# Last two layers with the gated-linear-attention block in the head, attention in finer steps, and other durations in the program's clock

## The chip, the cores and the metric

The kernel runs on 1 core of one Trainium2 chip, in one launch. The metric is device time in microseconds: the median of three runs before is 2298.22 us (2297.33 to 2300.84).

## The reference

Four layers over 256 tokens of width 1024. The first two (kind "a") have a mixer of four branches and a gated feed-forward part; the last two (kind "b") have another mixer, cross-attention to a memory, and a squared-ReLU part. What the change touches is the mixer of kind "b", and the attentions of both kinds:

```python
def mixer_block(h, ...):                      # kind "b", 256 tokens
    zin = h @ w_in
    (cq, ckv, kpe, sg_uv, gq, gk, gv, g_lr, g_og,
     dq, dk, dv, da, db, dz, gates) = jnp.split(zin, splits, axis=-1)
    o_a = mla_branch(cq, ckv, kpe, ...)       # causal attention, 4 heads
    o_b = spatial_gating_branch(sg_uv, ...)   # u * (tril(w_s) @ layernorm(v)), gelu before
    o_c = gla_branch(gq, gk, gv, g_lr, g_og, ...)   # gated linear attention, chunks of 64
    o_d = deltanet_branch(dq, dk, dv, da, db, dz, ...)
    branches = jnp.stack([o_a, o_b, o_c, o_d], axis=2)
    proj = jnp.einsum('bsnw,nwd->bsnd', branches, w_branch)
    gate = jax.nn.sigmoid(gates).reshape(b, s, N_BRANCH, D_MODEL)
    merged = jnp.sum(gate * proj, axis=2)
    return merged @ w_out
```

The mixer of kind "a" has a state-space branch and three softmax attentions of eight heads (fox, moba, dsa). Everything is in float32.

## The kernel before

Each large product is done in three: an fp32 operand is split into `hi` (rounded to fp32r) and `lo` (the rest), and TensorE multiplies lo x hi, hi x lo and hi x hi (`mm3`, L652). The small products of the branches are plain fp32 matmuls. Weights come in chunks of two 128-row tiles by up to 512 columns, 512 KB, in the order that `plan` (L67) lists and from which they are also laid out in memory. SyncE loads a chunk into one of 4 raw buffers (`load`, L486); `high` (L496) writes hi on ScalarE; `low` (L509) writes lo on VectorE, frees the raw buffer and asks for the next load. There are 8 pairs of hi and lo, and preparation runs at most 5 chunks ahead (`LOOK`).

The program writes out the order of all instructions of every engine itself; each engine then works through its own list in order. The main thread is the list of blocks of large products (`block`, `g1`, `g2`, `head`). Around it run lanes, Python generators, one for each branch ("A", "B", "C", "S", "X"), and short spawned chains such as an evacuation. A lane puts out instructions up to its next `yield`. The order comes from a model of the chip, a clock for each engine (`Model`, L303): `Engine.cost` (L372) gives each instruction a duration, `dma` (L428) gives one to a load, and a result can be read some 200 ns after its end. After 3 to 12 matmuls of the main thread `tick` (L635) is called. It puts out the next step of a lane when, by that clock, TensorE has come to the time at which the lane's last results are ready; lanes wait while VectorE or ScalarE is more than `BACKLOG` (2750 ns) behind TensorE. `advance` (L521), called in `tick`, puts out at most one `low` and one `high`: when the chunk is needed within 4000 ns of matmuls, or when the engine is not more than 1500 ns behind TensorE. The program is written twice; the first pass only finds when each chunk is needed. So other durations change the order and nothing else. `flush(key)` puts out all steps left of the chains with a key at once. Buffers of the branches are taken from an arena of 19968 words for each partition (`F`); when it is full, `relieve` puts out steps of other lanes early.

`attention` (L855) is one generator for all softmax attentions of a mixer. A step takes two heads: it multiplies the probabilities of the pair before last with v, transposes those of the last pair on TensorE and copies them to SBUF, multiplies q and k of this pair, reduces the rows on VectorE, takes exponentials on ScalarE, and then a reciprocal (128x4) and four multiplications on VectorE. There is one `yield` for each step.

In `layer_b` (L1635) the blocks are A (latents of the attention, low-rank gate, deltanet's scalars; 440 columns) and E (spatial gating, 512 columns), both in the head, and then those of `MORDER` (L64): B (keys and queries of gated linear attention, 256), qk (512), F (its values and output gates, 512), v (256) and dz (256). `head` (L714) works through the first 128 tokens of both blocks ahead of the second 128, since these are normalised meanwhile. After E each half gets `gelu` (L1739); lane "S" (`sgu`, L1765) first flushes these chains and then does spatial gating; lane "A" is `mla` with the attention of four heads; lane "C" is `gla` (L1813), set off after block F; lane "B" is deltanet (`dn`), set off after v. `gla` needs the low-rank gate first (softplus on VectorE), B's keys and queries then, and F's values only near its end, where it waits for `placed`. `mix` (L1400) then asks for the branches in the order 1 (spatial gating), 0, 2, 3 (`ORDER2`), with two gate blocks for each.

Of the kernel before, what the change touches and what calls it, by code (L numbers as in the profile page):

```python
# [59 lines left out]

ORDER1 = (2, 1, 3, 0)
ORDER2 = (1, 0, 2, 3)
MIDDLE = dict(B=("gq", "gk"), qk=("dq", "dk"), v=("dv",), F=("gv", "gog"), dz=("dz",))
MORDER = ("B", "qk", "F", "v", "dz")  # L64


def plan(layer):  # L67
# [33 lines left out]
            else:  # L101
                cb(f"d{j}{c}", "w_ffn_out", (l,), (256 * j, 256 * j + 256), [(c * 512, c * 512 + 512)])
    else:
        for name, parts in (("A", ("ckv", "kpe", "cq", "glr", "da", "db")), ("E", ("sg",)),
                            *((n, MIDDLE[n]) for n in MORDER)):
            cb(name, "w_in_2", (l,), full, [W2[p] for p in parts])
        g0 = W2["gates"][0]
# [244 lines left out]
class Engine:  # L352
# [19 lines left out]
    def cost(self, fn, outs, ins, kw):  # L372
        if self.name == "PE":
            if fn == "transpose":
                return 109.0
            m, n = ins[0].free_size(), ins[1].free_size()
            one = max(m / 1.2, n / 2.4) + 2
            return one if ins[0].dtype == F32R else max(112.0, max(2 * m / 1.2, 4 * n / 2.4))
        n = max(a.free_size() for a in outs[:1] + ins)
        psum = any("PSUM" in str(a.space) for a in ins + outs)  # L380
        ptr = sum(1 for a in ins if a.free_size() == 1) if n > 1 else 0
        if self.name == "ACT":
            return (94 if psum else 147) + n / 1.2 + 93 * (ptr + (len(outs) > 1))
        if self.name == "POOL":
            return 300 + 167 * n if kw.get("op") == OP.pow else 150 + 2.1 * n
        if fn in ("tensor_copy", "tensor_scalar", "memset") and not psum:
            return (n / 2 + 66) / 0.96 + 61 * ptr
        return (n + 66) / 0.96 + 61 * ptr + (1600 * n / 256 if fn == "reciprocal" else 0)


class Kern:
# [36 lines left out]
    def dma(self, out, in_):  # L428
        if self.due is not None:
            self.nc.sync.dma_start(out, in_)  # L430
        if "SB" in str(out.space):
            self.model.op("DMA", out.nbytes() / 360.0, 2000.0, [out], [])

    def act(self, out, in_, f=AF.Copy, scale=1.0, bias=None, accum=None):
        kw = {}
# [419 lines left out]
    def attention(self, heads, qk, sel, bias, v, dst, done):  # L855
# [16 lines left out]
        for i in range(n + 2):  # L872
# [15 lines left out]
            if 1 <= i <= n:  # L888
                ps, pts = st.pop(("p", i - 1)), []
                for p in ps:  # L890
                    b = self.bank()
                    for c in range(3):
                        self.tr(b[:, 128 * c:128 * c + 128], p.a[:, 128 * c:128 * c + 128])
                    pt = F.alloc(384, "pt")
                    self.copy(pt.a, b[:, :384])
                    self.fbank(b)
                    p.free()
                    pts.append(pt)
                st[("pt", i - 1)] = pts
            if i < n:  # L900
                qks = [qk(2 * i + j) for j in range(2)]
                bb = [self.bank() for _ in range(2)]
# [16 lines left out]
                for j in range(2):  # L919
                    for t, (a, c) in enumerate(tiles):  # L920
                        self.V.tensor_tensor_reduce(out=ps[j].a[:, a:c], in0=bb[j][:, 2 * a:2 * a + c - a], in1=bias[:, a:c],
                                                    scale=1.0, scalar=3e38, op0=OP.add, op1=OP.min,
                                                    accum_out=nv[:, 0, j, t:t + 1])
                    self.fbank(bb[j])
                    for t, (a, c) in enumerate(tiles):
                        self.act(ps[j].a[:, a:c], ps[j].a[:, a:c], AF.Exp, scale=-1.0, bias=nv[:, 0, j, t:t + 1],
                                 accum=nv[:, 1, j, t:t + 1])
                self.V.reciprocal(nm.a[:, 8:12], nm.a[:, 4:8])
                for j in range(2):
                    for t, (a, c) in enumerate(tiles):  # L930
# [704 lines left out]
    def layer_b(self, l, hT, nxt, pr, early):  # L1635
# [127 lines left out]
                bce.free()  # L1763

        def sgu():  # L1765
            self.flush("sg")
            m = Mat(self, 2, 256, "yT")
            for t in range(2):
                b = self.bank()
# [10 lines left out]
            ys[1].append(m)  # L1780
            flags.add(1)

        self.head(L, [("A", 440, ev_A), ("E", 512, ev_E)], hT)


        def convs(name, c0, n):
            for g in range(n):
# [2 lines left out]
                        [(256 * g, 256 * g + 128), (256 * g + 128, 256 * g + 256)], 4, g == n - 1)  # L1790
                self.spawn(self.conv(b, [cwt[:, c0 + 2 * g + j] for j in range(2)], None,
                                     cv.v(3, 512)[:, c0 // 2 + g]), "conv")
        self.lane("S", sgu())
        self.lane("A", mla())

        gq, gk = F.alloc(256, "gq"), F.alloc(256, "gk")
        def gate_ev(dst, b, src, norm):
            th = F.alloc(256, "gth")
# [10 lines left out]

        def ev_dz(t, b):  # L1810
            self.spawn(gate_ev(zg.v(2, 256)[:, t], b, b[:, 0:256], n_dn), "dz")

        def gla():  # L1813
            while len(given) < 2:
# [378 lines left out]

        cv = F.alloc(6 * 256, "cv")
        cvv = cv.v(6, 256)
        gv, gg, zg = F.alloc(512, "gv"), F.alloc(512, "gg"), F.alloc(512, "zg")
        for name in MORDER:
            if name == "qk":
                convs("qk", 0, 2)
# [2 lines left out]
            elif name == "B":  # L2202
                b = self.bank()
                self.g2([b[:, 0:256], b[:, 256:512]], L, "B", hT, [(0, 128), (128, 256)], 4)
                self.act(gq.a, b[:, 0:256], AF.Copy, scale=32 ** -0.5)
                self.act(gk.a, b[:, 256:512])
                self.fbank(b)
            elif name == "F":
                self.block(L, "F", hT, 512, ev_F)
                self.lane("C", gla())  # L2210
            else:
                self.block(L, "dz", hT, 256, ev_dz)
            placed.add(name)
# [467 lines left out]
```

## Time and profile before

| | us |
|---|---|
| median of the runs | 2298.22 |
| profiled execution, its own time | 2296.01 |
| its span, first to last instruction | 2294.2 |
| TensorE busy | 2237.2 |
| VectorE busy | 1526.5 |
| ScalarE busy | 1074.2 |
| GpSimd busy | 271.2 |
| mean granted TensorE clock | 0.991 |

PE is TensorE's matmuls, PEld its weight loads, DVE VectorE, ACT ScalarE, POOL GpSimd, SP SyncE. Nearly all instructions stand under line 362, the helper that issues them, so groups are told apart by tile names and shapes: `rt` holds split operands, `raw` weights as loaded, `ft` and `qt` the branches' buffers, `bank` PSUM. DVE `rt<-raw,rt` is `low`, ACT `rt<-raw` is `high`. A plain fp32 matmul stands as two records. Matmuls overlap in the pipeline, so the mean duration of one is longer than the time from one to the next. The first two layers take the span up to some 1149 us, the third starts there, and the last at some 1718 us.

### The profile page before, as it was taken

The numbers are of one execution on the slowest core, as the hardware profiler recorded it, in microseconds if no ns is written. First come the engines' busy times: TensorE is split into PE (matmuls) and PEld (weight loads), VectorE is DVE, ScalarE is ACT, GpSimd is POOL, SyncE is SP. The second block draws the span as 40 slices with busy tenths as digits, with TensorE's granted clock in tenths as the row PEclk, the third lists the DMA queues.
The fourth block names the chain that finished last, engine by engine and source line by source line (L and its number), as shares of the span: only waits on it lengthen the run. The fifth ranks groups of instructions, "written<-read, shape, count | busy, mean of one in ns | idle before, by whom it ended". The sixth has DMA issues, their size and how long they took to land.

```text
span 2294.2 us, 40097 instructions
## 1 busy us (share of the span) xinstructions
PE 2237.2 (98%) x16244; PEld 2020.1 (88%) x16244; DVE 1526.5 (67%) x2509; ACT 1074.2 (47%) x1695; POOL 271.2 (12%) x244
## 2 busy tenths in 40 slices
PE   7999999999999999999999999999999999999998
PEld 6888998999787899889988899988988889998897
DVE  7786657555888655755588867555557887755554
ACT  4554544444455444544454345444545433544543
POOL 3002120000301112000021321000002132000000
PEclk9999999999999999999999999999999999999999
DMA  6433555555534356565544246456653424644563
GB/s 224 140 122 118 184 183 194 198 182 168 174 118 147 110 166 202 174 228 187 171 132 155 86 131 218 144 177 221 195 165 113 156 94 136 214 155 157 193 204 108
DMA packets 106662, 375.47 MB, mean 164 GB/s; under 512 B 12474, under 2 KB 12908, under 8 KB 106476
## 3 DMA queue, kind: packets, MB, share of 16 engines
q1 hardware_dynamic: 106476, 372.91, 49.4%
q8 instruction: 127, 2.08, 0.4%
q14 instruction: 59, 0.48, 0.1%
HBM read 371.81 MB, written 1.05 MB: 163 GB/s over the span
## 4 chain that ended last, share of the span: by engine, by line
PE 63%; DVE 6%; issue 2%; ACT 1%; DMA 1%; POOL 1%; SPq 0%; POOLq 0%; DVEq 0%; ACTq 0%
PE bank L362 63%; DVE ft L362 4%; DVE rt L362 2%; POOL ft L362 1%; ACT rt L362 1%; ACT ft L362 0%; DMA raw<-in_wts_a 0%; DMA raw<-in_wts_b 0%; DMA ft<-in_positions 0%; POOL qt L362 0%; ACT junk L362 0%; SPq L430 0%; DVE junk L362 0%; POOLq L2676 0%; DVEq L362 0%
## 5 line engine op out<-in xcount | busy, mean ns | idle before, releaser
L362 PE MATMUL bank<-rt 128*128 128x256 f32 (+2 forms) x12720 | 1993.5, 316 | 28.0 <-DVE rt L362 27.7
L362 PEld LDWEIGHTS bank<-rt 128*128 128x128 f32 x12720 | 1781.1, 192 | 186.2 <-DVE rt L362 34.7
L362 DVE TENSOR_TENSOR rt<-raw,rt 128x1024 fp32r<-128x1024 f32 (+2 forms) x692 | 837.5, 1239 | 343.5 <-ACT rt L362 342.3
L362 ACT ACTIVATE rt<-raw 128x1024 fp32r<-128x1024 f32 (+2 forms) x692 | 698.7, 1034 | 410.4 <-PE bank L362 213.5
L362 POOL TENSOR_TENSOR ft<-ft 128x512 f32<-128x512 f32 (+7 forms) x186 | 213.1, 1153 | 1879.7 <-DVE ft L362 1673.5
L362 PE MATMUL bank<-ft 64*64 64x64 f32 (+11 forms) x3476 | 315.6, 266 | 18.8 <-DVE ft L362 12.0
L362 PEld LDWEIGHTS bank<-ft 64*64 64x64 f32 (+6 forms) x3476 | 243.7, 147 | 74.5 <-issue 16.0
L362 ACT ACTIVATE ft<-bank 128x512 f32<-128x512 f32 (+5 forms) x256 | 135.7, 536 | 317.6 <-PE bank L362 290.2
L362 ACT ACTIVATE ft<-ft 128x128 f32<-128x128 f32 (+7 forms) x206 | 87.5, 434 | 182.5 <-DVE ft L362 175.7
L362 DVE SCALAR_TENSOR_TENSOR ft<-ft 128x512 f32<-128x512 f32 (+5 forms) x211 | 93.6, 465 | 42.0 <-ACT junk L362 20.5
L362 DVE TENSOR_TENSOR ft<-ft 128x512 f32<-128x512 f32 (+5 forms) x122 | 68.3, 562 | 63.0 <-ACT ft L362 60.6
L362 DVE SCALAR_TENSOR_TENSOR ft<-bank,ft 128x254 f32<-128x254 f32 (+6 forms) x176 | 80.5, 482 | 24.5 <-PE bank L362 13.9
L362 ACT ACTIVATE rt<-bank 128x512 fp32r<-128x512 f32 (+1 forms) x98 | 53.6, 552 | 85.1 <-PE bank L362 84.1
L362 DVE TENSOR_TENSOR ft<-ft,bank 64x512 f32<-64x512 f32 (+3 forms) x92 | 59.3, 645 | 36.0 <-PE bank L362 29.6
L362 ACT ACTIVATE ft<-bank,ft 128x256 f32<-128x256 f32 x108 | 47.2, 481 | 72.0 <-PE bank L362 48.6
L362 DVE SCALAR_TENSOR_TENSOR ft<-ft,bank 128x512 f32<-128x512 f32 (+1 forms) x106 | 67.6, 642 | 14.6 <-PE bank L362 9.9
L362 DVE COPY ft<-bank 128x384 f32<-128x384 f32 (+6 forms) x96 | 49.4, 542 | 32.9 <-PE bank L362 30.4
L362 DVE TENSOR_SCALAR ft<-ft 128x256 f32<-128x256 f32 (+7 forms) x236 | 55.4, 277 | 21.3 <-ACT ft L362 9.8
L362 ACT ACTIVATE rt<-ft 128x512 fp32r<-128x512 f32 x62 | 39.0, 630 | 65.0 <-DVE ft L362 60.5
L362 DVE TENSOR_TENSOR ft<-bank,ft 128x512 f32<-128x512 f32 (+8 forms) x124 | 50.3, 442 | 16.1 <-PE bank L362 7.5
L362 POOL TENSOR_SCALAR qt<-qt,ft 64x256 fp32r<-64x256 f32 (+1 forms) x32 | 42.1, 1318 | 131.4 <-PE bank L362 130.5
L362 ACT ACTIVATE junk<-ft 128x512 bf16<-128x512 f32 (+1 forms) x46 | 27.2, 591 | 58.1 <-DVE ft L362 55.6
(37 smaller groups left out, 318.6 us busy)
## 6 DMA issues: line engine op xcount, KB each, us to landing
raw<-in_wts_a SPq DMA_DIRECT2D x340, 512.0 KB, 4.4
raw<-in_wts_b SPq DMA_DIRECT2D x312, 512.0 KB, 4.2
raw<-in_wts_b SPq DMA_DIRECT2D x24, 256.0 KB, 2.8
raw<-in_wts_b SPq DMA_DIRECT2D x8, 440.0 KB, 4.2
raw<-in_wts_a SPq DMA_DIRECT2D x8, 340.0 KB, 5.1
ft<-in_mem SPq DMA_DIRECT2D x4, 512.0 KB, 8.3
ft<-in_x SPq DMA_DIRECT2D x2, 512.0 KB, 3.4
ft<-in_norm_mix_pre SPq DMA_DIRECT2D x2, 512.0 KB, 5.3
```

What stands on the lines that cost most here:

```text
L362: r = None if self.dry else f(*args, **kw)
```

## The change

In the last two layers block F goes into the head in E's place, and E takes F's kind of place, behind B: the order A, E, B, qk, F, v, dz becomes A, F, B, E, qk, v, dz. `gla` is set off behind B, `sgu` behind E; `sgu` waits in a loop of `yield` until the gelu chains are through, where it flushed them. `attention` gets two more `yield`: one behind the copies of the transposed probabilities, one behind the exponentials. In the program's clock a split matmul gets a longer duration, small fp32 matmuls a shorter one, and a load a higher rate with a longer latency.

```diff
-MIDDLE = dict(B=("gq", "gk"), qk=("dq", "dk"), v=("dv",), F=("gv", "gog"), dz=("dz",))
-MORDER = ("B", "qk", "F", "v", "dz")
+MIDDLE = dict(B=("gq", "gk"), qk=("dq", "dk"), v=("dv",), E=("sg",), dz=("dz",))
+MORDER = ("B", "E", "qk", "v", "dz")
@@ def plan(layer):
-        for name, parts in (("A", ("ckv", "kpe", "cq", "glr", "da", "db")), ("E", ("sg",)),
+        for name, parts in (("A", ("ckv", "kpe", "cq", "glr", "da", "db")), ("F", ("gv", "gog")),
@@ def cost(self, fn, outs, ins, kw):
-            m, n = ins[0].free_size(), ins[1].free_size()
-            one = max(m / 1.2, n / 2.4) + 2
-            return one if ins[0].dtype == F32R else max(112.0, max(2 * m / 1.2, 4 * n / 2.4))
+            rows, m, n = ins[0].shape[0], ins[0].free_size(), ins[1].free_size()
+            if ins[0].dtype == F32R:
+                return max(m / 1.2, n / 2.4 + 12) + 1.5
+            if rows <= 64 and m <= 64:
+                return 68.0
+            share = 0.67 if min(rows, m) <= 64 else 1.0
+            return share * 2 * max(m / 1.2 + 1, n / 1.2 + 2)
@@ def dma(self, out, in_):
-            self.model.op("DMA", out.nbytes() / 360.0, 2000.0, [out], [])
+            self.model.op("DMA", out.nbytes() / 400.0, 2900.0, [out], [])
@@ def attention(self, heads, qk, sel, bias, v, dst, done):
                 st[("pt", i - 1)] = pts
+                yield
             if i < n:
...
                         self.act(ps[j].a[:, a:c], ps[j].a[:, a:c], AF.Exp, scale=-1.0, bias=nv[:, 0, j, t:t + 1],
                                  accum=nv[:, 1, j, t:t + 1])
+                yield
                 self.V.reciprocal(nm.a[:, 8:12], nm.a[:, 4:8])
@@ def sgu():
-            self.flush("sg")
+            while "sg" in self.keys.values():
+                yield
@@ def layer_b(self, l, hT, nxt, pr, early):
-        self.head(L, [("A", 440, ev_A), ("E", 512, ev_E)], hT)
...
-        self.lane("S", sgu())
-        self.lane("A", mla())
...
+        gv, gg = F.alloc(512, "gv"), F.alloc(512, "gg")
+        self.head(L, [("A", 440, ev_A), ("F", 512, ev_F)], hT)
+        placed.add("F")
+        self.lane("A", mla())
...
-        gv, gg, zg = F.alloc(512, "gv"), F.alloc(512, "gg"), F.alloc(512, "zg")
+        zg = F.alloc(512, "zg")
         for name in MORDER:
...
                 self.fbank(b)
-            elif name == "F":
-                self.block(L, "F", hT, 512, ev_F)
                 self.lane("C", gla())
+            elif name == "E":
+                self.block(L, "E", hT, 512, ev_E)
+                self.lane("S", sgu())
```

## Rows read from the trace of the kernel before

**Rows 1.** The page, busy time of TensorE: us, share of the span, instructions.

```profile
PE 2237.2 (98%) x16244; PEld 2020.1 (88%) x16244; DVE 1526.5 (67%) x2509; ACT 1074.2 (47%) x1695; POOL 271.2 (12%) x244
```

**Rows 2.** TensorE's timeline, a stretch at full clock: start us, us, operation, count.

```profile
414.03 10.20 PE L362 MATMUL bank<-rt 128*128 128x256 f32 x83
```

**Rows 3.** What TensorE waited for: us in total, times, longest us.

```profile
PE bank L362 <- DVE rt L362: 27.7, 20, 3.1
PE bank L362 <- DVE ft L362: 12.0, 6, 7.4
PE bank L362 <- POOL ft L362: 6.4, 10, 1.8
PE bank L362 <- POOL qt L362: 3.4, 2, 1.7
```

**Rows 4.** TensorE's timeline, first and last of the four waits, in brackets.

```profile
128.85 2.36 PE L362 MATMUL bank<-rt 128*128 128x256 f32 x10 [3.03 <-DVE rt L362]
...
806.12 1.65 PE L362 MATMUL bank<-rt 128*128 128x256 f32 x6 [3.10 <-DVE rt L362]
```

**Rows 5.** Windows, TensorE alone: stretch, length, busy (count), granted clock, DMA.

```profile
129.70:133.00 3.30, 3.18 (x16) 0.50 0.90 282
400.00:410.00 10.00, 9.22 (x42) 1.00 0.34 107
805.60:812.20 6.60, 6.08 (x28) 0.50 0.24 79
1252.70:1256.00 3.30, 3.14 (x16) 0.50 0.84 254
1822.70:1826.00 3.30, 3.30 (x15) 0.50 0.90 295
```

**Rows 6.** TensorE's timeline in the last two layers.

```profile
1251.78 0.98 PE L362 MATMUL bank<-rt 128*128 128x256 f32 x6 [1.91 <-DVE rt L362]
...
1821.50 0.97 PE L362 MATMUL bank<-rt 128*128 128x256 f32 x6 [1.90 <-DVE rt L362]
```

**Rows 7.** VectorE's timeline ahead of the first wait.

```profile
123.23 1.01 DVE L362 COPY ft<-bank 128x384 f32<-128x384 f32 x2
124.17 0.28 DVE L362 CUSTOM_DVE_ANT_0 ft<-bank,ft 128x128 f32<-128x128 f32 x1
...
126.44 0.18 DVE L362 RECIPROCAL ft<-ft 128x4 f32<-128x4 f32 x1 [1.09 <-ACT ft L362]
126.66 1.01 DVE L362 TENSOR_SCALAR ft<-ft 128x128 f32<-128x128 f32 x4
127.58 2.36 DVE L362 TENSOR_TENSOR rt<-raw,rt 128x1024 fp32r<-128x1024 f32 x2
```

**Rows 8.** Groups by shape: operation, shapes, count, busy, mean ns, idle before.

```profile
L362 DVE RECIPROCAL ft<-ft 128x4 f32<-128x4 f32 x28 | 5.0, 178 | 30.3 <-ACT ft L362 30.3
```

**Rows 9.** TensorE's timeline, a short wait.

```profile
400.78 0.97 PE L362 MATMUL bank<-rt 128*128 128x512 f32 x3 [1.35 <-DVE rt L362]
```

**Rows 10.** TensorE's timeline, a break in the split matmuls.

```profile
1313.21 0.98 PE L362 MATMUL bank<-rt 128*128 128x256 f32 x6
1314.12 0.47 PE L362 MATMUL bank<-ft 32*64 32x64 f32 x16
```

**Rows 11.** VectorE's timeline in gated linear attention.

```profile
1220.30 1.75 DVE L362 RECIPROCAL ft<-ft 128x256 f32<-128x256 f32 x1
```

**Rows 12.** Window of all engines, third layer's blocks.

```profile
1200.00:1210.00 10.00, 10.00 (x55) 8.60 (x54) 7.64 (x27) 5.83 (x18) 0.00 (x0) 1.00 0.00 1
```

**Rows 13.** Timeline of all engines, GpSimd beside `low` and alone.

```profile
171.70 2.11 POOL L362 TENSOR_TENSOR ft<-ft 128x512 f32<-128x512 f32 x1 [47.59 <-DVE ft L362]
...
173.79 2.61 POOL L362 TENSOR_SCALAR qt<-qt,ft 32x128 fp32r<-32x128 f32 x1
...
176.46 0.38 PE L362 MATMUL bank<-qt 32*128 32x256 f32 x1 [1.68 <-POOL qt L362]
...
177.40 1.28 POOL L362 TENSOR_TENSOR ft<-ft 128x512 f32<-128x512 f32 x1 [0.99 <-DVE ft L362]
```

## The prediction

> **What bounds the kernel now.** I read the page's busy times first, then TensorE's waits, then its timeline at the waits, last the granted clock there. TensorE is busy for 2237.2 of 2294.2 us [rows 1], and what it does at full clock is fixed by the shapes: 83 split matmuls of 128x256 take 10.20 us [rows 2], about 0.12 us each. The change removes no matmul. So it can only act on the time in which TensorE waits or runs at the lower clock. The waits are small: 27.7 us on VectorE's weight preparation, 12.0 us on other VectorE work, 6.4 and 3.4 us on GpSimd [rows 3], 49.5 us together. Four waits of 3.0 to 3.1 us (the first and the last stand in [rows 4]) make up 12.3 of the 27.7 us. Behind most long waits the clock goes down: after the one that ends at 128.85 the granted clock is 0.50 (1.2 GHz) from 129.7 to 133.0, after the one at 806.12 for 6.6 us [rows 4, 5]; in all it does so behind three of the four, and behind the waits of 1.9 us that end at 1251.78 and 1821.50 [rows 5, 6]. In 3.3 us at 0.50 TensorE did 15 to 16 matmuls [rows 5] where 27 fit at full clock (3.3 / 0.12); such a stretch costs some 1.3 us (11 x 0.12).
>
> Why these four waits? In front of the first, VectorE does an attention step: two copies (123.23), four row reductions (124.17 on), then it stands still for 1.09 us until ScalarE's exponentials are done, then one reciprocal and four multiplications (126.44 to 127.58), and only then the `low` halves of two weight chunks, for the first of which TensorE is waiting [rows 7]. The order is written by the program: an attention step goes out in one piece, so `low` can't come between. Each of the 28 head pairs has this standstill, 30.3 us of idle VectorE in all [rows 8]; it costs TensorE time only where a weight chunk stands behind it. The four waits have the same order of VectorE work ahead of them.
>
> **The change part by part.** The sum is made against the profiled execution, 2296.0 us (span 2294.2 and 1.8 around it); the median of the runs is 2298.2, 2.2 us above it.
>
> *Finer attention steps.* The first new `yield` lets `low` go between the copies and the reductions, the second between the exponentials and the reciprocal. In the rows the second place alone puts the first `low` at about 125.35 and not 127.58: 2.2 us sooner, of which 1.09 us was standstill. A wait of 3.1 us becomes 0.9 us. Behind the wait of 1.35 us that ends at 400.78 the clock stays full [rows 5, 9], so I also take away the four stretches of 1.3 us that follow three of the four waits (one, one, and at 805.6 two). Gain: 4 x 2.2 + 4 x 1.3 = 14.0 us. The bounds: nothing, if other VectorE work takes the freed place; 12.3 + 5.2 = 17.5 us, if no wait is left. I take 14.0, which follows from the rows themselves.
>
> Against it, the first `yield` cuts a step's TensorE part in two (transposes ahead, scores behind): 3 more breaks in each of six attentions of eight heads, 1 in each of two with four heads, 20 in all. Where such a break stands now, six split matmuls from 1313.21 to 1314.12 take 0.91 us, not 6 x 0.12 = 0.72 [rows 10]: 0.19 us a break. Bounds 0 (two steps may still go out behind each other) and 3.8 us; I take 3.
>
> *Last two layers.* The projected gated-linear-attention values and gates take the place of spatial gating in the head; both blocks are 512 wide, so TensorE's blocks only change places, and the weight chunks are loaded in the new order at the same size. The lane of gated linear attention starts after the third block and not after the fifth, 2 x 96 x 0.12 = 23 us sooner. Its first part loads VectorE with softplus on 256 columns, its reciprocal alone 1.75 us at 1220.30, with a dozen smaller operations over the same columns [rows 11]. Today that lies where the deltanet lane sets in too, and behind both is the wait of 1.91 us that ends at 1251.78, in the second layer 1.90 us at 1821.50 [rows 6]. With their two stretches at 0.50 these cost 1.91 + 1.90 + 2.6 = 6.4 us. Moved forward, that part falls on a stretch where VectorE is busy for 7.64 of 10 us [rows 12], so it has 2.4 us in ten to give, and the gating's gelu, which leaves the head, falls there too. So I count half, 3.2 us, with bounds of a loss of the same 6.4 us (new waits of this kind there, the old ones left) and a gain of 6.4. Nothing later depends on it: spatial gating is asked for first in the merge, but three blocks of projection and one of gates still lie between. The wait in the gating lane (a `yield` loop in place of `flush`) costs TensorE nothing: `flush` put out the rest of gelu at once, now it goes out as it gets ready, and no one is queued behind it. One price is in the program's memory: the gating's buffers (1024, 896 and 512 words) live longer while gated linear attention takes its own, in an arena of 19968 words. If it runs out, the program forces out steps early; I count 0 for it and at most some 4 us (as many early steps, each for 1 us of waiting).
>
> *Durations in the program's clock.* These are numbers by which the program orders instructions, and no work. For a split matmul of 128x256 the old number is 108.7 ns, the new one 120.2, and the rows have 0.12 us [rows 2]; small matmuls become cheaper (112 to 68 ns). Until now TensorE in the program's clock was up to 10% too fast, so each lane's next step was put behind 10% more matmuls than its wait called for: a hidden margin, 0.3 to 0.8 us for waits of 3 to 8 us. It goes. In return preparation is put out sooner, since VectorE now seems less far behind. GpSimd's numbers stay, and they are short: 1225 ns for 128x512, where the rows have 1.28 us alone, but 2.11 us while VectorE does `low`, and 2.61 us for 32x128, for which the program counts 419 ns; one wait of 1.68 us came from it [rows 13]. A larger DMA number (2900 ns latency) holds ScalarE's `high` back in the program's clock; the ScalarE engine has the room. Value: a loss of 2 us; bounds: a gain of 6.0 us (both waits of this kind, 3.4, with 1.3 behind each) and a loss as in the second rival.
>
> The Trainium skill (SBUF — State Buffer, "Who interferes with whom") says that a VectorE instruction with two inputs in SBUF keeps a GpSimd instruction that reads SBUF out of their shared port until it is done. The trace agrees (2.11 against 1.28 us, beside `low` work) [rows 13], and the rule speaks against this change: more `low` between small steps means more GpSimd steps of the longer kind. By this rule the second rival is what comes out.
>
> Sum: -14.0 + 3 - 3.2 + 2 = -12.2 us, so 2283.8 us for a profiled execution and 2286.0 us for the median.
>
> **The rivals.** (1) *Given back.* VectorE, not the order of one step, is what is short at these places; the freed 2.2 us are taken by the next lane, and a wait of 3 us stands elsewhere. For it: lanes go out until VectorE is 2750 ns behind in the program's clock, whatever the step's size. Against it: the standstill of 1.09 us is real idle time. The time: of the 14.0 us the filled standstill alone is left (4 x 1.09), against 5 us for breaks and late steps: near 2298.
>
> (2) *Slower: TensorE comes too early to GpSimd's results.* The place: the steps in which TensorE reads what GpSimd wrote, some 56 (20 rotary additions, 24 gate rows in the first two layers, 12 level products in the last two). For it: the margin that goes is about what GpSimd's numbers lack beside `low` (2.11 - 1.28 = 0.83 us). Against it: now only 12 such waits, 9.8 us. If a third of the steps (19) wait for 0.8 us more, that is 15 us; with half of the gain on attention left (-7) and the breaks (+3), the median is 2309. It decides from where TensorE's waits on GpSimd pass some 25 us.
>
> (3) *More than forecast.* All named waits go, those on GpSimd's rows with their two stretches too: -17.5 - 6.4 - 6.0 = -29.9, so 2268. For it: the new numbers are nearer to the rows. Against it: GpSimd's are not touched.
>
> **How the numbers follow.** Forecast (2277 to 2293) 0.45; more than forecast (below 2277) 0.17; given back (2293 to 2303) 0.20; slower by GpSimd (above 2303) 0.18. Range 2268 to 2304, which leaves out some 0.1 at each end. A difference of 0.2% (4.6 us) is about what a measurement tells from none: faster than 2293.6 has the forecast, the third rival and a little of the first, 0.63; slower than 2302.8 has 0.18; 0.19 is left.
>
> **What would show it.** Right: no wait of over 2 us on weight preparation in the stretches of attention, the idle time ahead of the 28 reciprocals well below 30.3 us, a granted clock of 1.00 behind them, TensorE's waits on VectorE's preparation near 17 us and not 27.7; in the last two layers no wait of 1.9 us in the first two gates, and VectorE fuller before the third projection. Wrong: waits of the old length at new places (first rival), or waits on GpSimd of 25 us and more (second).

## The result: 2282.46 us, and the profile after

The changed kernel takes 2282.46 us (median of five runs, 2281.47 to 2290.12) against 2298.22 (five, 2297.33 to 2300.90): ratio 0.9942, 95% interval 0.9922 to 0.9963. Ratio and interval go by all executions, not by the medians alone (their quotient is 0.9931): three executions of the changed kernel lie at 2281.47 to 2282.46 us and two at 2289.37 and 2290.12. The forecast was 2286.0. The profiled execution takes 2281.47 us, its span is 2279.7. One execution of the last experiment below, e12_steps8_F, took 5277.41 us and is left out of its ratio; without it its median is 2283.82 and not 2283.93.

TensorE's busy time after (answering [rows 1]):

```profile
PE 2232.7 (98%) x16244; PEld 2015.1 (88%) x16244; DVE 1526.0 (67%) x2509; ACT 1073.2 (47%) x1695; POOL 267.0 (12%) x244
```

49.5 us of TensorE's waits [rows 3] became 39.6: 20.4 on weight preparation, 13.5 on other VectorE work, 5.7 on GpSimd. That small difference hides a larger gain and a loss, which a cut at the third layer's first projection shows. Windows of before, then of after (stretch, length, busy and count of PE, PEld, DVE, ACT and POOL, granted clock, DMA share, GB/s); the first row is the first two layers, the second the last two:

```profile
10.40:1149.60 1139.20, 1109.56 (x7496) 999.26 (x7497) 767.54 (x1342) 540.56 (x874) 135.78 (x101) 0.99 0.51 168
1149.60:2294.20 1144.60, 1125.68 (x8741) 1019.28 (x8740) 755.11 (x1161) 529.31 (x815) 134.66 (x138) 0.99 0.48 158
```

```profile
10.00:1127.60 1117.60, 1102.96 (x7496) 994.73 (x7496) 770.91 (x1343) 540.42 (x875) 130.12 (x101) 1.00 0.53 172
1127.60:2279.70 1152.10, 1127.78 (x8740) 1018.78 (x8740) 751.31 (x1159) 528.85 (x815) 136.10 (x138) 0.99 0.48 156
```

The first two layers became 21.6 us shorter, the last two 7.5 us longer. What TensorE waited for in the two parts of the span before (us in total, times, longest us):

```profile
PE bank L362 <- DVE rt L362: 21.4, 11, 3.1
PE bank L362 <- POOL ft L362: 3.5, 4, 1.8
PE bank L362 <- POOL qt L362: 3.4, 2, 1.7
PE bank L362 <- DVE ft L362: 2.1, 3, 1.2
```

```profile
PE bank L362 <- DVE rt L362: 6.4, 9, 1.9
PE bank L362 <- POOL ft L362: 2.9, 6, 0.7
PE bank L362 <- DVE ft L362: 2.6, 2, 1.7
```

And after:

```profile
PE bank L362 <- DVE rt L362: 7.5, 6, 2.5
PE bank L362 <- DVE ft L362: 5.0, 3, 4.1
PE bank L362 <- POOL ft L362: 2.6, 4, 1.2
```

```profile
PE bank L362 <- DVE rt L362: 12.9, 10, 4.2
PE bank L362 <- POOL ft L362: 3.0, 3, 1.2
PE bank L362 <- DVE ft L362: 1.1, 4, 0.3
```

In the first two layers the waits sum to 15.1 us after, where before they were 30.4; in the last two to 17.0 against 11.9. (The rest, some 7 us of one wait, stands ahead of the first matmul.) The mean granted clock went from 0.99 to 1.00 in the first part.

**Where attention gained.** VectorE after, at the place of [rows 7] (start us, us, operation, count):

```profile
117.99 1.01 DVE L362 COPY ft<-bank 128x384 f32<-128x384 f32 x2
118.92 1.22 DVE L362 TENSOR_TENSOR rt<-raw,rt 128x1024 fp32r<-128x1024 f32 x1
120.05 2.94 DVE L362 SCALAR_TENSOR_TENSOR ft<-bank,ft 128x255 f32<-128x255 f32 x6
122.91 0.28 DVE L362 CUSTOM_DVE_ANT_0 ft<-bank,ft 128x128 f32<-128x128 f32 x1
...
127.56 2.94 DVE L362 SCALAR_TENSOR_TENSOR ft<-bank,ft 128x255 f32<-128x255 f32 x6 [3.47 <-ACT ft L362]
```

Between the copies at 117.99 and the row reductions at 122.91 now stand one `low` and six convolution steps of another lane: the first new `yield` at work. VectorE then stands still for 3.47 us, longer than the 1.09 of before, and nobody waits for it: TensorE does 83 split matmuls in a row from 121.02 in 10.22 us, as at full clock [rows 2].

```profile
121.02 10.22 PE L362 MATMUL bank<-rt 128*128 128x256 f32 x83
```

Ahead of the reciprocals [rows 8] there is no idle time left (busy, mean ns, idle before); a standstill like that of 3.47 us now stands ahead of whatever lane's work comes next. What VectorE waits for ScalarE's `ft` results in all fell from 145.3 to 116.5 us, so most of the standstills are filled and not only moved.

```profile
L362 DVE RECIPROCAL ft<-ft 128x4 f32<-128x4 f32 x28 | 4.8, 170 | 0.0
```

Beside the four waits of 3.0 to 3.1 us in attention, the kernel before has a fifth, in the second layer's feed-forward part; a stretch at 0.50 follows it. It is 1.76 us after, and 2.15 in e3 below, whose order there is that of before, so not all of what it lost is shown to come from the change:

```profile
1002.60 1.61 PE L362 MATMUL bank<-rt 128*128 128x256 f32 x9 [3.14 <-DVE rt L362]
```

**Where the last two layers lost.** All engines after, at the end of the third layer's projections; the last layer repeats it at 1779.98:

```profile
1202.49 3.69 DVE L362 SCALAR_TENSOR_TENSOR ft<-bank,ft 128x64 f32<-128x64 f32 x10
...
1206.11 0.68 DVE L362 SCALAR_TENSOR_TENSOR ft<-ft 128x512 f32<-128x512 f32 x1
...
1206.71 1.82 DVE L362 TENSOR_TENSOR rt<-raw,rt 128x512 fp32r<-128x512 f32 x2
...
1207.44 1.86 PE L362 MATMUL bank<-rt 128*128 128x256 f32 x7 [4.17 <-DVE rt L362]
```

Ten operations stand in the line at 1202.49, which names the shape of the first: four of spatial gating (128x64) and six convolution steps of up to 128x255. They and one of 128x512 go ahead of the `low` at 1206.71, and TensorE waits 4.17 us for that `low`. The waits of 1.91 and 1.90 us [rows 6] are gone; two of 4.17 us have come, ahead of the gate blocks. The loss lies there: from the third layer's start to its first gate block it takes 85.4 us after and 79.0 before, from there to the third branch's projection 127.7 and 128.7.

### The profile page after: what moved, and what is told of

The parts are those of the page before. It is cut to its first block, busy times and chain, and to the rows that moved or that the text cites. A ratio compares the mean times of both kernels' runs of the same rounds, so it can differ in the third digit from the quotient of the medians.

```text
span 2279.7 us, 40153 instructions
## 1 busy us (share of the span) xinstructions
PE 2232.7 (98%) x16244; PEld 2015.1 (88%) x16244; DVE 1526.0 (67%) x2509; ACT 1073.2 (47%) x1695; POOL 267.0 (12%) x244
## 3 DMA queue, kind: packets, MB, share of 16 engines
q8 instruction: 127, 2.08, 0.4%
## 5 line engine op out<-in xcount | busy, mean ns | idle before, releaser
L362 PE MATMUL bank<-rt 128*128 128x256 f32 (+2 forms) x12720 | 1996.2, 316 | 20.5 <-DVE rt L362 20.4
L362 POOL TENSOR_TENSOR ft<-ft 128x512 f32<-128x512 f32 (+6 forms) x186 | 213.0, 1154 | 1847.4 <-DVE ft L362 1578.0
L362 PE MATMUL bank<-ft 64*64 64x64 f32 (+13 forms) x3476 | 312.9, 264 | 19.6 <-DVE ft L362 13.5
L362 PEld LDWEIGHTS bank<-ft 64*64 64x64 f32 (+6 forms) x3476 | 240.3, 146 | 78.1 <-DVE ft L362 19.6
L362 ACT ACTIVATE ft<-bank 128x512 f32<-128x512 f32 (+4 forms) x256 | 135.2, 536 | 305.2 <-PE bank L362 292.5
L362 DVE SCALAR_TENSOR_TENSOR ft<-bank,ft 128x255 f32<-128x255 f32 (+6 forms) x176 | 80.2, 482 | 26.5 <-PE bank L362 10.0
L362 DVE COPY ft<-bank 128x384 f32<-128x384 f32 (+5 forms) x96 | 49.3, 541 | 31.4 <-PE bank L362 28.7
L362 DVE SCALAR_TENSOR_TENSOR rt<-bank,rt 128x512 fp32r<-128x512 f32 (+1 forms) x72 | 43.3, 612 | 17.2 <-ACT rt L362 17.0
```

The costliest lines, as they stand in the source:

```text
L362: r = None if self.dry else f(*args, **kw)
```

## The experiments

Each part alone, two of the three pairs (blocks with durations was not run), and the parts of the parts. Each is timed beside the kernel before on the same chip, which took 2298.39 us beside e1 to e4, 2297.67 beside e5 to e8 and 2299.77 beside e9 to e12. The table is the map for what follows. "First" and "last" are the lengths of the first and last two layers in the profiled execution, cut as above; "waits" are TensorE's, "low" the time at a granted clock of 0.50 (its last stretch, at the program's end, left out), both for first / last; "p20" is the time from the end of the third branch's gate block (g20) to the start of its projection (p20), in the third layer. All columns behind the ratio come from one execution each. How far one differs from the next shows in kernels whose edits leave the first two layers alike: 1114.4, 1112.3, 1112.2 and 1113.8 us in e1, e5, e10 and e12, and 1117.6, 1120.3 and 1120.3 in the changed kernel, e4 and e8. Differences below some 3 us in these columns say nothing.

| kernel | median us | ratio, 95% interval | first | last | waits | low | p20 |
|---|---|---|---|---|---|---|---|
| before | 2298.22 | 1 | 1139.2 | 1144.6 | 30.4 / 11.9 | 23.9 / 13.7 | 0.2 |
| after | 2282.46 | 0.9942 (0.9922 to 0.9963) | 1117.6 | 1152.1 | 15.1 / 17.0 | 10.2 / 17.1 | 0.1 |
| e1_steps | 2288.78 | 0.9957 (0.9942 to 0.9973) | 1114.4 | 1162.3 | 13.0 / 19.6 | 6.8 / 37.5 | 0.1 |
| e2_clock | 2320.21 | 1.0098 (1.0080 to 1.0116) | 1133.3 | 1175.0 | 27.4 / 30.6 | 6.8 / 34.1 | 15.9 |
| e3_blocks | 2311.89 | 1.0071 (1.0052 to 1.0091) | 1138.6 | 1161.9 | 28.0 / 17.2 | 23.9 / 30.7 | 0.1 |
| e4_steps_clock | 2305.95 | 1.0034 (1.0020 to 1.0049) | 1120.3 | 1173.7 | 16.6 / 28.0 | 13.7 / 37.5 | 15.6 |
| e5_steps8 | 2273.61 | 0.9896 (0.9881 to 0.9911) | 1112.3 | 1146.3 | 12.3 / 14.8 | 3.4 / 13.7 | 0.3 |
| e6_split | 2301.09 | 1.0012 (1.0001 to 1.0023) | 1140.2 | 1151.9 | 28.9 / 14.5 | 20.5 / 20.5 | 0.1 |
| e7_small | 2308.13 | 1.0039 (1.0026 to 1.0052) | 1137.4 | 1156.5 | 29.1 / 20.1 | 13.7 / 20.5 | 15.9 |
| e8_after_steps8 | 2314.95 | 1.0076 (1.0061 to 1.0091) | 1120.3 | 1187.0 | 17.5 / 34.6 | 10.2 / 47.8 | 0.1 |
| e9_clock_F | 2326.68 | 1.0110 (1.0090 to 1.0129) | 1135.7 | 1179.9 | 27.5 / 32.4 | 10.2 / 41.0 | 15.4 |
| e10_steps_blocks | 2291.87 | 0.9967 (0.9955 to 0.9979) | 1112.2 | 1167.4 | 13.9 / 23.1 | 3.4 / 30.7 | 0.1 |
| e11_dma | 2332.71 | 1.0139 (1.0122 to 1.0156) | 1145.1 | 1175.0 | 35.9 / 34.4 | 13.7 / 30.7 | 10.1 |
| e12_steps8_F | 2283.93 | 0.9928 (0.9912 to 0.9944) | 1113.8 | 1158.5 | 12.3 / 20.4 | 6.8 / 20.5 | 0.3 |

### The parts alone, and two together

*e1_steps*: the two `yield` in `attention`, nothing else of the change.

> Only the two new yields in attention; block order and durations as before. Theory: the four waits of 3 us in the first two layers lose 2.2 us each and their four stretches at the lower clock go, against 20 breaks: -14 + 3, a median near 2287, and the last two layers stay within 2 us of before. Rival (the durations remove these waits, the steps don't): the four waits stay above 2 us and the median is 2296 or more.

*e2_clock*: the durations of matmuls and loads, nothing else.

> Only the durations in the program's clock (matmuls and loads); attention steps and block order as before. Theory: a loss of some 2 us, TensorE waiting a little more on GpSimd (above 9.8 us), the four waits of 3 us still there: a median near 2300. Rival: preparation goes out sooner and the four waits go without finer steps: 2288 or less.

*e3_blocks*: block order, lanes and the gating's loop, nothing else.

> Only the order of the blocks in the last two layers, with the lanes' starts and the waiting loop of spatial gating; steps and durations as before. Theory (from the changed kernel's trace, in which the last two layers take 7.7 us more): the new order itself makes VectorE late on weights behind the v block, a wait of some 4 us in each of the two layers with a low clock behind it: a median near 2305. Rival (the new durations pack VectorE too full there): with the old durations the new order costs nothing or gains, 2292 to 2298.

*e4_steps_clock*: e1's edit and e2's.

> Finer steps and new durations, with the old block order in the last two layers. Theory: the first two layers are those of the changed kernel, 22 us less than before, and the last two those of before: a median near 2276, 6 us below the changed kernel. Rival (the new durations cost the last two layers 7 us in either order): a median near 2283, as the changed kernel.

The edit of e1, and in e4 beside that of e2:

```diff
                 st[("pt", i - 1)] = pts
+                yield
...
+                yield
                 self.V.reciprocal(nm.a[:, 8:12], nm.a[:, 4:8])
```

e2 has the hunks of `cost` and `dma` of the change as they stand, e3 those of `MIDDLE`, `plan`, `sgu` and `layer_b`, with

```diff
-MORDER = ("B", "qk", "F", "v", "dz")
+MORDER = ("B", "E", "qk", "v", "dz")
```

Measured against before: steps alone -9.6 us, durations alone +21.8, blocks alone +13.5; together the three give -15.8. They do not add. Of the four expectations only that for e1 met the time (2288.78 for 2287), by a gain more than twice as large and a loss that it did not have; e2, e3 and e4 are 20, 7 and 30 us above theirs, and above their rivals' as well. The wait of some 4 us behind the v block that e3 was to show is not there; its longest in the last two layers is 2.46 us, in other blocks. The steps gain 24.8 us in the first two layers and lose 17.7 in the last two. The durations and the blocks do little in the first two and each lose in the last two, 30.4 and 17.3 us.

Little on the whole is not little in the parts. With the durations alone the four waits of 3 us [rows 4] are gone or below 2 us as well, as the rival for e2 had it. But a new one has come where the second layer starts, 4.01 us in e2, and the changed kernel has it too; before, the longest there is 1.14 us:

```profile
579.80 1.75 PE L362 MATMUL bank<-ft 128*128 128x128 f32 x8 [4.08 <-DVE ft L362]
```

What the durations do in the last two layers stands between g20 and p20 (TensorE's timeline in e2; idle time before and its end in brackets):

```profile
1348.91 1.84 PE L362 MATMUL bank<-ft 128*64 128x64 f32 x24
1351.89 1.62 PE L362 MATMUL bank<-ft 128*64 128x64 f32 x22 [1.15 <-DVE ft L362]
1355.56 0.44 PE L362 MATMUL bank<-ft 128*128 128x128 f32 x2 [2.05 <-DVE ft L362]
1356.65 3.55 PE L362 MATMUL bank<-ft 128*128 128x128 f32 x22 [0.65 <-DVE ft L362]
1363.40 0.69 PE L362 MATMUL bank<-ft 128*128 128x128 f32 x2 [3.20 <-DVE ft L362]
1364.56 2.75 PE L362 MATMUL bank<-rt 128*128 128x256 f32 x10 [0.47 <-ACT rt L362]
```

g20 is through at 1348.7, and then TensorE has nothing but small matmuls of the lanes, most of them waiting for VectorE: 7.52 us of waits in 15.9 us. The merge asks for gated linear attention at p20, it is not done, and `mix` puts out steps of all lanes (`drain`) until it is. In the kernel before the same small matmuls stand between split ones:

```profile
1354.13 0.38 PE L362 MATMUL bank<-ft 128*128 128x128 f32 x2
1354.26 3.11 PE L362 MATMUL bank<-rt 128*128 128x256 f32 x24
1357.21 0.38 PE L362 MATMUL bank<-ft 128*128 128x128 f32 x2
1357.35 2.88 PE L362 MATMUL bank<-rt 128*128 128x256 f32 x22
```

Gated linear attention's last matmul there is at 1354.13, 3.2 us ahead of p20's first at 1357.35, (the two at 1357.21 are deltanet's), and VectorE writes the low half of its result from 1354.96 to 1355.38, 2.0 us ahead. That is all the margin there was. Of the 18.7 us of waits that e2 adds in the last two layers, 14.5 are of this kind (17.1 us on VectorE's lane results against 2.6); with them comes more time at 0.50.

### Eight heads or four

*e5_steps8*: the kernel before with the two `yield` for eight heads only, so in the first two layers.

> Finer steps only where attention has eight heads (the first two layers); durations and block order as before. Theory: the steps' gain of 25 us in the first two layers stays, and their loss of 18 us in the last two comes from the four-head attention, which they draw out from 43 to 71 us into the time of the other lanes: a median near 2274. Rival (the last two layers lose by something else, as the order of everything behind shifts): a median near 2289, as with finer steps everywhere.

*e8_after_steps8*: the changed kernel with the same condition.

> The changed kernel, with the finer steps only for eight heads. Theory: the four-head attention ends some 25 us earlier and leaves VectorE to gated linear attention and spatial gating, so the wait of 4.2 us behind the v block goes in both of the last layers: a median near 2275. Rival (that wait comes from softplus and gelu there, not from attention): it stays above 2.5 us, and the median is 2280 or more.

```diff
                 st[("pt", i - 1)] = pts
-                yield
+                if heads == 8:
+                    yield
...
-                yield
+                if heads == 8:
+                    yield
                 self.V.reciprocal(nm.a[:, 8:12], nm.a[:, 4:8])
```

e5 came out as expected, 2273.61 us: the gain of the first two layers (-26.9 us) with next to no loss in the last two (+1.7). So the steps' loss in e1 is that of the four-head attention. There its matmuls run from 1151.4 to 1222.5 in e1 and from 1174.8 to 1218.3 before, 71 us and not 43. One place of e1, in the middle of that stretch (all engines):

```profile
1196.99 1.75 DVE L362 RECIPROCAL ft<-ft 128x256 f32<-128x256 f32 x1
...
1199.73 2.93 DVE L362 SCALAR_TENSOR_TENSOR ft<-bank,ft 128x255 f32<-128x255 f32 x6
...
1202.57 2.95 DVE L362 TENSOR_TENSOR rt<-raw,rt 128x512 fp32r<-128x512 f32 x3
...
1203.31 3.99 PE L362 MATMUL bank<-rt 128*128 128x256 f32 x17 [2.47 <-DVE rt L362]
```

VectorE does a reciprocal of gated linear attention (1.75 us) and six convolution steps (2.93 us) with one short `low` between them, and TensorE waits 2.47 us. That the drawn-out attention brings such places about is a reading of the trace; e5 shows that the loss goes with the four-head steps, not by which way.

e8 failed the expectation: in the changed kernel the coarse four-head steps cost 32.5 us by the medians (2314.95 against 2282.46). Spatial gating's matmuls run from 1220.0 to 1238.1 in e8 and from 1186.9 to 1218.2 in the changed kernel, and its projection starts at 1240.7, behind the last of them; there (e8, VectorE, then TensorE):

```profile
1245.47 0.42 DVE L362 SCALAR_TENSOR_TENSOR rt<-bank,rt 128x256 fp32r<-128x256 f32 x1
...
1245.94 1.44 PE L362 MATMUL bank<-rt 128*128 128x256 f32 x5 [4.86 <-DVE rt L362]
```

The operation at 1245.47 writes the gating's result, not a weight: the projection waits 4.86 us for the gating itself, and its first block takes from 1240.7 to 1252.4 where in the changed kernel it takes 2.8 us. The last layer has the same wait. In the block in which the changed kernel waits 4.17 us, the longest waits of e8 are 2.35 and 2.96 us, so that these waits are only in part the gain that was expected.

So the four-head steps cannot be called good or bad: they cost 16 us in the last two layers with the old order and durations (e1 against e5) and save 34.9 us there with the new (after against e8). Nor are they what draws the attention out there: its matmuls run for 72 us in e8 and for 75 in the changed kernel. Why the gating is put out 29 us later in e8, counted from the layer's start, lies in the program's order of lanes, and was not tried further.

### Which duration, and whether the start of the lane decides

*e6_split*: only the split matmul's duration. *e7_small*: only the small fp32 matmuls'. *e11_dma*: only the load's. *e9_clock_F*: all of them (e2), and block F behind B, so that gated linear attention starts sooner.

> Of the durations only the split matmul's (108.7 to 120.2 ns for 128x256); small matmuls and loads as before. Theory: what costs 30 us in the last two layers is that gated linear attention is not through when its projection p20 is due (15 us of TensorE between g20 and p20 in each), and that comes from the shorter small matmuls, so here p20 follows g20 at once: a median of 2290 to 2300. Rival (the slower split matmul makes the lanes late): a break of some 15 us ahead of p20, 2310 or more.

> Of the durations only those of plain fp32 matmuls (112 to 68 ns for the small ones); split matmuls and loads as before. Theory: TensorE's clock in the program moves less in each step of the two recurrent lanes, so more split matmuls are put between two of their steps, and p20 waits for gated linear attention by some 15 us in each of the last two layers: a median of 2315 or more. Rival (the split matmul's number does it): p20 follows g20 at once, 2300 or less.

> The kernel before with the new durations, and in the last two layers the values and gates F placed straight behind B instead of behind qk; spatial gating stays in the head. Gated linear attention can start some 14 us sooner than with the durations alone. Theory (what costs is that g20 is through before gated linear attention, whenever that began): in the order that the program writes, about 6 us of TensorE's lane work still stand between g20 and p20, so p20 again starts 13 to 17 us behind g20's end, the last two layers are 20 to 30 us longer than before, 2312 to 2322 us. Rival (the late start of gated linear attention is the cause): p20 follows g20 within 6 us, 2292 to 2302 us.

> Only the transfer's duration in the program's clock changed (400 bytes per ns and 2900 ns behind them instead of 360 and 2000), TensorE's durations and all else as before. Theory (any duration that lets the gate blocks run ahead of gated linear attention costs a break at p20): about 6 us of lane work stand between g20 and p20 in the order written, p20 starts 12 to 16 us behind g20's end, the last two layers 12 to 25 us longer, 2308 to 2322 us. Rival (the transfer's duration was the harmless one of the three, and the loss with all of them comes from the matmuls' alone): 2295 to 2302 us.

The edits of e6, e7 (only lines that it adds; its `m, n` and the F32R line are left out), e9 (beside e2's) and e11:

```diff
-            one = max(m / 1.2, n / 2.4) + 2
-            return one if ins[0].dtype == F32R else max(112.0, max(2 * m / 1.2, 4 * n / 2.4))
+            if ins[0].dtype == F32R:
+                return max(m / 1.2, n / 2.4 + 12) + 1.5
+            return max(112.0, max(2 * m / 1.2, 4 * n / 2.4))
```

```diff
+            if rows <= 64 and m <= 64:
+                return 68.0
+            share = 0.67 if min(rows, m) <= 64 else 1.0
+            return share * 2 * max(m / 1.2 + 1, n / 1.2 + 2)
```

```diff
-MORDER = ("B", "qk", "F", "v", "dz")
+MORDER = ("B", "F", "qk", "v", "dz")
```

```diff
-            self.model.op("DMA", out.nbytes() / 360.0, 2000.0, [out], [])
+            self.model.op("DMA", out.nbytes() / 400.0, 2900.0, [out], [])
```

The split matmul's number is near harmless (+3.4 us by the medians; 2301.09 is just above the lower of the two ranges expected). The small matmuls' costs 10.5 us, the load's 32.9, more than all three together (21.8). e7 fell between its two expectations: the break at p20 is there, 15.9 us long, but its gate blocks had run ahead of before (g20 is through 197.6 us after the third layer's start, before 207.5), so of the break the waits are lost (+8.2 us in the last two layers) and little else. e11 has a break, as its theory said, but a shorter one (10.1 us for 12 to 16), and its time is 10 us above the range: TensorE waits for VectorE's preparation all over the span. In e11:

```profile
PE bank L362 <- DVE rt L362: 50.2, 44, 5.6
```

The waits for `low` are 50.2 us against 27.7 [rows 3], and ScalarE stands idle ahead of `high` for loads for 226.6 us against 188.5. A reading that fits: with a later landing in the clock the `high` and `low` of a chunk go out later, its raw buffer comes free later, and so the next load is asked for later. That chain was not tried by itself.

e9 answered its question: gated linear attention started at 1197.0 of a third layer that starts at 1145.8 (before: 1214.4 of 1149.6), 13.6 us sooner, and the break is as long as in e2, as the theory said; the time, 2326.68 us, and the last two layers, 35.3 us longer, lie above its ranges. The start of the lane does not decide whether there is a break; where its last steps are put, against the gate blocks, does.

### The pair left over, and an early F with the old durations

*e10_steps_blocks*: the changed kernel with the old durations. *e12_steps8_F*: e5 with e9's `MORDER`.

> Finer attention steps in all layers and the moved blocks, with the old durations (the changed kernel without its durations). Theory (the new durations bring nothing of their own once blocks are moved and steps are fine): no break ahead of p20, first two layers 22 to 26 us shorter than before, last two 8 to 18 us longer, 2280 to 2292 us. Rival (the parts add up with the old durations: -9.6 for the steps, +13.5 for the blocks): 2298 to 2306 us; then it takes the new durations too to get to 2282.

> Old durations, finer steps for eight heads alone, and F straight behind B with spatial gating still in the head. Theory (starting gated linear attention early costs nothing as long as p20 finds it done; here no lane work stands between g20 and p20): 2270 to 2278 us, as with the finer steps for eight heads alone (2273.6). Rival (an early gated linear attention takes VectorE from the four-head attention and from the weights' preparation, as when the blocks were moved alone, +13.5): 2281 to 2290 us, with waits above 2 us on VectorE in the first two gate blocks of the last two layers.

e10 lies in its theory's range on the whole (2291.87), but not by layer: the first two gain 27.0 us and the last two lose 22.8, where 26 and 18 were the most allowed. Against it the changed kernel is 5.4 us longer in the first two layers and 15.3 shorter in the last two. So the new durations, which lose 21.8 us alone and 17 with the steps (e4 against e1), no longer lose once blocks and steps are both changed: by the medians they gain 9 us, but the two intervals overlap (0.9922 to 0.9963, 0.9955 to 0.9979), so a gain is not shown. e12's theory fell and its rival came: 2283.93, 10.3 us above e5, with the last two layers 12.2 us longer and a wait above 2 us in the first gate block. The early start costs though p20 finds all done. The first gate block's first weights in e12 (all engines):

```profile
1203.42 2.94 DVE L362 SCALAR_TENSOR_TENSOR ft<-bank,ft 128x255 f32<-128x255 f32 x6 [2.08 <-ACT ft L362]
...
1206.28 4.62 DVE L362 TENSOR_TENSOR rt<-raw,rt 128x1024 fp32r<-128x1024 f32 x4
...
1207.55 0.98 PE L362 MATMUL bank<-rt 128*128 128x256 f32 x6 [2.42 <-DVE rt L362]
```

VectorE has stood still for 2.08 us, takes the convolutions first, and TensorE waits 2.42 us for the first of four `low`. In e5 the gate block starts without such a wait and has one of 3.46 us later; its waits sum to 14.8 us, e12's to 20.4.

**A version that beats both.** e5: 0.9896 (0.9881 to 0.9911) against 0.9942 (0.9922 to 0.9963) for the change; the intervals do not meet. TensorE's waits in its first two layers:

```profile
PE bank L362 <- DVE rt L362: 7.2, 7, 1.4
PE bank L362 <- POOL ft L362: 3.7, 4, 2.0
PE bank L362 <- DVE ft L362: 1.4, 3, 0.8
```

## Why the prediction was right on the sum, and where not

- *What bounds the kernel.* Right. TensorE's work stayed (2237.2 and 2232.7 us), and the change acted on waits and on the clock behind them.
- *Finer attention steps, -14.0 (at most -17.5), breaks +3.* Right in mechanism, too small in size. With the steps alone the first two layers became 24.8 us shorter, with e5 26.9: waits -18.1 us and 20.5 us less at 0.50. All four waits went whole (12.3 us), not 2.2 us of each, and with them both waits for `qt` (3.4 us) that I had put under the durations. The fifth, at 1002.60, I had not counted. All seven stretches at 0.50 behind these went and one came, where I had counted on four. What the 20 breaks at 0.19 us cost was not measured by itself.
- *The four-head attention.* The step that failed. I counted its two breaks at 0.4 us; alone, its finer steps cost 16 us in the last two layers (e1 against e5), and in the whole change they save 34.9 there (e8 against the changed kernel). So a term that I had at nearly nothing is among the largest, and its sign hangs on the order and the durations beside it.
- *Last two layers, -3.2 (bounds of 6.4 either way).* Wrong in sign and size: +17.3 us alone (e3), +7.5 for the two layers with all parts. The window at 1200 to 1210 [rows 12], with VectorE busy for 7.64 us of ten, was no measure of room: TensorE waited for one `low` with eleven operations in front of it. The two 1.9 us waits went, as forecast, and two of 4.17 us came, which the blocks alone do not bring (e3 has none above 1 us behind v; with the steps, in e10, they are 3.11 and 2.22). "Nothing later depends on it" was wrong too: in e8 the gating's projection starts 2.6 us behind the gating's last matmul.
- *Durations, +2.* Far off as a part by itself: +21.8 us. The mechanism I named for a loss, waits for GpSimd (second rival), is not it: they are 8.0 us in e2 and 5.7 in the changed kernel, 9.8 before. What lost most was gated linear attention at p20, which I had not looked at: its margin of 3.2 us was in the trace. The load's number, which I priced at nothing because ScalarE has room for a later `high`, is the dearest of the three alone (+32.9), with 22.5 us more of waits for `low`; by which way is not shown. In the whole change the term is no loss (after against e10), and whether it is a gain is open.
- *The sum.* In the profiled executions -14.5 us came for a forecast of -12.2. That it came so near is luck: a gain in the first two layers some 10 us larger than counted met a loss in the last two that was not counted, and the three parts alone, forecast at -11.0, -3.2 and +2, measured -9.6, +13.5 and +21.8. *Given back* happened, but in the last two layers only; the gain of attention in the first two passed my upper bound for it, 17.5 us.
- *What would show it.* The waits of over 2 us on preparation are gone from the stretches of the eight-head attentions, the idle time ahead of the reciprocals went to 0.0, and the clock there is full. The two waits of 4.17 us, with time at 0.50, stand in the stretches of the four-head attention; with them TensorE's waits on preparation are 20.4 us and not near 17. VectorE was to be fuller before the third projection and was not: from the first gate block to it, it is busy for 95.1 of 127.7 us, before for 101.9 of 128.7.

## What to carry to other kernels

Cutting a step where an engine stands still inside it lets other lanes' work in between. For the attentions of eight heads that was worth 25 to 27 us; for those of four heads the same cut lost 16 us with the old order and durations and saved 35 with the new. So try such a cut for each kind of layer by itself, beside the other changes with which it is to stand. In a kernel whose order is planned, measure every part alone and in pairs: the parts here were -9.6, +21.8 and +13.5 us, and -15.8 together. And before changing what sets the order, look for the smallest margin at a join in the main thread: here 3.2 us ahead of p20, and the five kernels that lost it are 11.9 to 35.3 us longer in the last two layers. A join can be lost elsewhere too: e8, the longest there (+42.4), kept p20's and lost the gating's.

## What the runs showed of the hardware

In most cases a wait gained or lost moved the time by more than its length. Against before, the last two layers of twelve of the thirteen kernels changed by 1.4 to 3.3 times what their waits changed (e11 +30.4 with +22.5, e3 +17.3 with +5.3); e5's +1.7 is within what one execution differs from another. What the length changes beyond the waits is 0.4 to 0.8 of the change in time at a granted clock of 0.50 (1.2 GHz): e1, last two layers, +17.7 us with +7.7 of waits and +23.9 at 0.50; e8, +42.4 with +22.7 and +34.1; e5, first two, -26.9 with -18.1 and -20.5. It holds in the first two layers only where the steps are finer: in e2, e7, e9 and e11 the time at 0.50 fell there by 10 to 17 us, and the length by at most 3 us beyond the waits. Why is open.

The length of a wait alone does not tell whether the clock falls. The same wait of 1.36 and 1.35 us ahead of the same matmuls (e12, then the changed kernel):

```profile
943.39 1.35 PE L362 MATMUL bank<-rt 128*128 128x512 f32 x3 [1.36 <-DVE rt L362]
```

```profile
947.27 0.97 PE L362 MATMUL bank<-rt 128*128 128x512 f32 x3 [1.35 <-DVE rt L362]
```

TensorE's windows right behind it, in the same order (busy and count, granted clock, DMA share, GB/s):

```profile
943.80:947.20 3.40, 3.40 (x11) 0.50 0.00 0
```

```profile
947.60:951.00 3.40, 3.40 (x17) 1.00 0.00 0
```

11 matmuls at 0.50 against 17 at 1.00.

A duration nearer to the trace need not give a better order. A load of 512 KB lands 4.4 us after its issue by the median (before):

```profile
raw<-in_wts_a SPq DMA_DIRECT2D x340, 512.0 KB, 4.4
```

The old number for it, when nothing stands ahead of it in the program's clock, is 3.46 us (524288 / 360 + 2000 ns), the new one 4.21; alone, the nearer one cost 32.9 us.
